# A group of seven products for chunk c3 of the first feed-forward's up projection, with the row sums, gates and tables moved around it

## The chip, the cores and the metric

The kernel runs on one core of a Trainium2 chip. The metric is the device time of one execution in microseconds (us). For the kernel before, three runs gave 896.94, 897.80 and 899.82 us; their median is 897.8 us. A further execution was taken with the hardware profiler; it took 896.07 us, and all views of the profile come from it.

## What is computed

The reference is a trunk of two layers over 256 rows of 1024 channels, in fp32. Each layer adds half a SwiGLU feed-forward, then a token mixer (a convolution module in the first layer, latent attention in the second), then half a second feed-forward:

```python
def swiglu_ffn(h, w1, w3, w2):
    return (jax.nn.silu(h @ w1) * (h @ w3)) @ w2
...
    h = h + FFN_RES_WEIGHT * swiglu_ffn(rmsnorm(h, ffn_norm1[i]), ffn1_w1[i], ffn1_w3[i], ffn1_w2[i])
    m = rmsnorm(h, mix_norm[i])
```

There are four feed-forwards, of which the change touches the first. Its first product, called up here, multiplies 256x1024 rows by w1 and by w3, each 1024x2816; its second product, called down, multiplies 256x2816 gates by w2, 2816x1024.

## The kernel before, in words

**The arithmetic.** TensorE multiplies in a reduced fp32 format, so that every operand is split in a high and a low part, and each product is made of three matmuls: `mm3` issues, in this order, the high part of the rows by the low part of the weights (L332), high by high (L335) and the low part of the rows by the high part of the weights (L336). ScalarE makes the high part of a weight (a copy that rounds), VectorE the low part (the raw weight less the high part).

**The weights.** They come from memory as blocks of 1 MB, 128 partitions by 2048 numbers, in the order of the list `blocks`. `load` fetches a block through SyncE's queue into one of four raw buffers (`RAW_BUFS`, pool `raw`; issue at L238), casts the high part in two halves on ScalarE (L246) and subtracts for the low part in two halves on VectorE (L247), into one of five pairs of weight buffers (`W_BUFS`). A raw buffer is free again when its low part is made. `weights` asks for the block that is used next, and `load_ahead` keeps a few blocks under way. `behind` holds these casts behind the last few instructions that are marked `urgent` on the same engine, and `order(a, b)` puts instruction a behind b; beyond that, the scheduler of the framework sets each engine's order when the program is built, and each engine, and SyncE's queue of transfers, works through its own order.

**The up projection** runs in chunks c0 to c5 (`ffn_in`, loop over c). A chunk yields 512 columns of w1 and of w3 for both halves of the rows (tb 0 and 1): four banks of 128x512, four weight blocks, 96 matmuls of 128x512 (c5 has half of that). Blocks are numbered b0, b1, ... here: c1 uses b4 to b7, c2 b8 to b11. Behind a chunk come its gates: Silu on ScalarE (L956), the product with the other bank on VectorE (L958, or L258 where it is `urgent`), and `turn`: VectorE transposes within 32x32 squares (L478), four transfers write the result to device memory (L482, gd<-gt) and one reads it back turned (L487, rows<-gd or gb<-gd), ScalarE and VectorE split it into the gates Gh and Gl (L853). The gates of c0 and c1 are read back into the tile `rows4`.

**A group of seven.** A chunk that stands in `SEVEN_UP` makes its 2x2 blocks of product (two halves of the rows, two halves of the inner dimension, w1 and w3) from seven block products instead of eight. It is Strassen's scheme in the form of Winograd. For it the rows need four sums and differences, `sums_of_rows` (L344 on VectorE), of rows that `whole_rows` puts together from high and low part first (L349, into a raw buffer), and each of them is split again by `forms_of` (L361 on ScalarE, L364 on VectorE). The weights need four differences of raw blocks, 128x2048 each, on VectorE (L200, raw<-raw,raw); `load_seven` fetches the four raw blocks (L184), makes these differences, the high halves (L214) and the low halves (L200, lo<-raw,hi). `seven_products` issues the seven products of 12 matmuls; between them it copies two banks (L258 on ScalarE) and makes two additions on VectorE (L258, u<-u,p), which are `urgent`. Its products are called first to seventh here; the fifth adds to the bank that the first addition reads. In the kernel before, c3 of the second, third and fourth feed-forward are such groups, and in all four feed-forwards the first four block columns of down are one (`SEVEN_DOWN`, `o.seven`), whose row sums are taken from `rows4`, that is from the gates of c0 and c1.

**Around it in the first feed-forward.** `diagonals` is a generator whose steps `beside` calls between products: it makes the convolution's diagonal matrices on ScalarE, 128x64 at a time (L1679, dpair). `rope_tables` makes sines and cosines of the positions on VectorE (L1366 and after) and ScalarE (L1398 to L1400), for the attention of the second layer. `Plain` makes the rows for the convolution behind down: squares (L429), a Sigmoid of one column (L669), which brings the table of that function in ahead of its use, and the scaling (L678).

## Time and profile before

| what | us |
|---|---|
| median of three runs | 897.8 |
| profiled execution, own time | 896.07 |
| its span (first to last instruction) | 894.3 |
| VectorE, busy | 743.1 |
| ScalarE, busy | 571.8 |
| low halves of ordinary blocks (L247), 236 of them, busy | 276.2 |
| low halves of groups (L200), 98 of them, busy | 115.6 |
| differences of raw blocks (L200), 28 of them, busy | 63.9 |

The span is taken from the trace; 1.77 us of the execution's own time lie around it. In the profile an engine is named PE (TensorE), DVE (VectorE), ACT (ScalarE), POOL (GpSimd) or SP (SyncE). A row of a timeline has the start in us from the span's beginning, the duration, engine, line and operation, the tile written and the tiles read, the size, and, where the engine was idle before it, the idle time and what ended it. "x2" stands for two instructions in one row. Durations of neighbours overlap a little, so the distance of two starts tells what an instruction costs in a full queue. A row of the windows has the busy time of each engine in a stretch, its number of instructions, and the clock that TensorE was granted (1.00 is full).

### The profile page before, as it was taken

What the parts mean: (1) busy time and instruction counts of PE and PEld (TensorE: products, weight loads), DVE (VectorE), ACT (ScalarE), POOL (GpSimd) and SP (SyncE); (2) the same over time, 40 slices, a digit from 0 to 9 for tenths busy, and PEclk for the clock granted to TensorE, in tenths of its full rate; (3) what the DMA queues carried; (4) which work ended last, traced back from release to release, by engine and by line L of the source; (5) the groups of instructions that cost most, each with busy time, mean ns of one, the idle gap of its engine ahead of it and who ended that gap; (6) DMA issues with size and microseconds to landing.
All of it is one profiled execution on the core that took longest, in us unless ns stands there. A gap on an engine that the chain in (4) does not pass through costs nothing.

```text
span 894.3 us, 12241 instructions
## 1 busy us (share of the span) xinstructions
PE 886.9 (99%) x4221; PEld 745.9 (83%) x4221; DVE 743.1 (83%) x1083; ACT 571.8 (64%) x993; POOL 104.2 (12%) x227
## 2 busy tenths in 40 slices
PE   9999999999999999999999999999999999999997
PEld 7888888898988888888888888888899888888886
DVE  6787789579998999999588989995768579989973
ACT  7966458488886646667375566673677566474752
POOL 1000000069962000000010000001400010000000
PEclk9999999999999999999999999999999999999999
DMA  9987629834215864939759369495635349378541
GB/s 330 375 303 274 232 59 355 295 121 172 106 60 194 289 258 144 374 109 388 259 175 339 118 218 357 123 392 182 223 142 189 141 154 342 104 260 317 180 196 48
DMA packets 71055, 198.94 MB, mean 222 GB/s; under 512 B 12369, under 2 KB 41937, under 8 KB 51665
## 3 DMA queue, kind: packets, MB, share of 16 engines
q1 hardware_dynamic: 70560, 197.47, 61.8%
q8 instruction: 33, 0.54, 0.2%
q10 hardware_dynamic: 432, 0.69, 0.2%
q14 instruction: 30, 0.24, 0.1%
HBM read 181.87 MB, written 16.25 MB: 222 GB/s over the span
## 4 chain that ended last, share of the span: by engine, by line
PE 92%; DVE 4%; ACT 2%; DMA 1%; issue 0%; SPq 0%; POOL 0%; DVEq 0%; ACTq 0%
PE u L336 16%; PE u L335 16%; PE u L332 16%; PE o L335 9%; PE o L336 9%; PE o L332 9%; PE gate L1005 2%; PE u L411 2%; DVE acc L1094 2%; PE u L1005 2%; PE tp L446 1%; PE a L335 1%; PE a L332 1%; PE a L336 1%; PE nope L336 1%; PE nope L332 1%
## 5 line engine op out<-in xcount | busy, mean ns | idle before, releaser
L247 DVE TENSOR_TENSOR lo<-raw,hi 128x1024 fp32r<-128x1024 f32 (+1 forms) x236 | 276.2, 1212 | 38.8 <-ACT hi L246 37.6
L246 ACT CAST hi<-raw 128x1024 fp32r<-128x1024 f32 (+1 forms) x238 | 236.8, 1044 | 89.3 <-DMA raw<-in_f2w 30.8
L332 PE MATMUL u<-lo,Xh 128*128 128x512 f32 x612 | 238.4, 389 | 0.1
L336 PE MATMUL u<-hi,Xl 128*128 128x512 f32 x612 | 238.3, 389 | 0.0
L335 PE MATMUL u<-hi,Xh 128*128 128x512 f32 x612 | 238.1, 389 | 0.0
L332 PEld LDWEIGHTS u<-lo,Xh 128*128 128x128 f32 x612 | 114.9, 188 | 24.5 <-ACT Xh L598 0.5
L336 PEld LDWEIGHTS u<-hi,Xl 128*128 128x128 f32 x612 | 114.9, 188 | 24.3 <-DVE Xl L465 0.5
L335 PEld LDWEIGHTS u<-hi,Xh 128*128 128x128 f32 x612 | 114.9, 188 | 23.8
L214 ACT CAST hi<-raw 128x1024 fp32r<-128x1024 f32 x98 | 97.7, 1050 | 51.8 <-DVE raw L200 44.9
L200 DVE TENSOR_TENSOR lo<-raw,hi 128x1024 fp32r<-128x1024 f32 x98 | 115.6, 1216 | 7.1 <-ACT hi L214 7.1
L332 PE MATMUL o<-lo,Gh 128*128 128x512 f32 (+1 forms) x276 | 106.6, 386 | 0.0
L335 PE MATMUL o<-hi,Gh 128*128 128x512 f32 (+1 forms) x276 | 106.5, 386 | 0.0
L336 PE MATMUL o<-hi,Gl 128*128 128x512 f32 (+1 forms) x276 | 106.5, 386 | 0.0
L437 POOL TENSOR_TENSOR ms<-ss 128x1 f32<-128x1 f32 x16 | 8.1, 510 | 597.6 <-ACT junk L429 597.6
L200 DVE TENSOR_TENSOR raw<-raw,raw 128x2048 f32<-128x2048 f32 x28 | 63.9, 2283 | 1.8 <-DMA raw<-in_f2w 0.9
L332 PEld LDWEIGHTS o<-lo,Gh 128*128 128x128 f32 x276 | 51.8, 188 | 10.5
L335 PEld LDWEIGHTS o<-hi,Gh 128*128 128x128 f32 x276 | 51.9, 188 | 10.5
L336 PEld LDWEIGHTS o<-hi,Gl 128*128 128x128 f32 x276 | 51.8, 188 | 10.4
L1094 DVE SCALAR_TENSOR_TENSOR acc<-V,dw,acc 128x128 f32<-128x128 f32 (+1 forms) x174 | 53.9, 391 | 0.0
L1115 ACT ACTIVATE prod<-V,dw 128x128 f32<-128x128 f32 (+1 forms) x128 | 45.6, 415 | 1.8 <-POOL Y L1116 1.0
L956 ACT ACTIVATE s<-u,R 128x512 f32<-128x512 f32 (+1 forms) x48 | 30.9, 647 | 24.8 <-PE u L336 24.1
L797 DVE SCALAR_TENSOR_TENSOR h<-o,rh,h 128x512 f32<-128x512 f32 (+1 forms) x18 | 12.9, 719 | 29.2 <-PE o L336 29.2
(265 smaller groups left out, 1257.7 us busy)
## 6 DMA issues: line engine op xcount, KB each, us to landing
raw<-in_f2w SPq DMA_DIRECT2D x66, 1024.0 KB, 6.2
raw<-in_f1w SPq DMA_DIRECT2D x62, 1024.0 KB, 6.5
raw<-in_cw SPq DMA_DIRECT2D x12, 1024.0 KB, 5.5
gd<-gt SPq DMA_DIRECT2D x160, 64.0 KB, 3.0
gb<-gd SPq DMA_DIRECT2D x24, 256.0 KB, 2.8
rows<-gd SPq DMA_DIRECT2D x16, 256.0 KB, 4.4
raw<-in_wo SPq DMA_DIRECT2D x4, 1024.0 KB, 4.9
hd<-rows SPq DMA_DIRECT2D x56, 64.0 KB, 2.4
```

Source lines behind the costliest of these rows:

```text
L200: ins = nc.vector.tensor_sub(out, left, right)
L214: casts[n, i] = nc.scalar.copy(hi[:, c], raw[:, c]), sub(lo[:, c], raw[:, c], hi[:, c].bitcast(F32))
L246: casts[len(loaded), i] = (nc.scalar.copy(hi[:, c], raw[:, c]), low.tensor_sub(lo[:, c], raw[:, c], hi[:, c].bitcast(F32)))
L247: low.tensor_sub(lo[:, c], raw[:, c], hi[:, c].bitcast(F32)))
L332: mm = nc.tensor.matmul(o, ah, bl, start=start, stop=False, skip_group_check=seeded)
L335: nc.tensor.matmul(o, ah, bh, start=False, stop=False, skip_group_check=seeded)
L336: return nc.tensor.matmul(o, al, bh, start=False, stop=stop, skip_group_check=seeded)
L411: mm = nc.tensor.matmul(o, al if kind == "x" else ah, bl if kind == "l" else bh, start=start and n == 0, stop=stop and n == len(kinds) - 1)
L956: nc.scalar.activation(s[:, :w], u[0, tb][:, :w], AF.Silu, scale=X.r[tb])
L1005: mm = nc.tensor.matmul(u[:, t], w[:, c], X.x[:, k, t], start=(k == 0), stop=(k == KT - 1))
L1094: dve_last.append(nc.vector.scalar_tensor_tensor(out if j == j1 - 1 else y, v, w, y, op0=ALU.mult, op1=ALU.add))
L1115: prods_last.append(nc.scalar.activation(p, v, AF.Copy, scale=w))
```

## The change

c3 of the first feed-forward becomes a group of seven (`SEVEN_UP[0]`), so it has 84 matmuls instead of 96. With it go:

- `whole_rows` is called at c1 for the first feed-forward, as for the others (two chunks ahead of the group), and there it stands behind the last low half of block b5 (`after`). The forms are kept in the part of Gh and Gl that later chunks fill.
- The row sums of the down group and its first form are made ahead of the group at c3 in the first feed-forward (`down`), instead of at c5.
- The gates of c2's first half of the rows (tb 0) are not held behind the group's copy and addition there (`held`); those of the second half are, as in the other groups, and their low part also stands behind the seventh product's.
- Each diagonal stands behind the latest high half that has been issued.
- `rope_tables` is no longer called behind the third feed-forward (from where the scheduler had placed its instructions in the first feed-forward's up projection), but as the last step of `diagonals`; its first instruction stands behind a low half of a block of down. The Sigmoid of `Plain` stands behind its last sine.

```diff
@@ -46,7 +46,7 @@
 
 
 
-SEVEN_UP = {1: (3,), 2: (3,), 3: (3,)}
+SEVEN_UP = {0: (3,), 1: (3,), 2: (3,), 3: (3,)}
 SEVEN_DOWN = (0, 1, 2, 3)
 
 CONV_DVE = (0, 2, 4)
@@ -344,9 +344,11 @@
             nc.vector.tensor_tensor(out, left, right, op=op)
         return sorted(((n, out) for n, out, *_ in sums), key=lambda s: s[0])
 
-    def whole_rows(xh, xl):
+    def whole_rows(xh, xl, after=()):
         x = rawp.tile([P, HB], F32, tag="raw", name=uid("xs")).rearrange("p (k t) -> p k t", t=S)
-        nc.vector.tensor_add(x, xh.bitcast(F32), xl.bitcast(F32))
+        whole = nc.vector.tensor_add(x, xh.bitcast(F32), xl.bitcast(F32))
+        for a in after:
+            order(whole, a.ins)
         return [x[:, 4 * a:4 * a + 4, tbs(tb)] for tb in range(2) for a in range(2)]
 
     def forms_of(sums, sh, sl, late={}):
@@ -365,7 +367,7 @@
             out[n] = [z[:, i].rearrange("p (k t) -> p k t", t=P) for z in (sh, sl)]
         return out
 
-    def seven_products(xh, xl, forms, banks, late={}):
+    def seven_products(xh, xl, forms, banks, late={}, held=True):
 
 
         def rows(a, tb):
@@ -393,8 +395,10 @@
         add = urgent(nc.vector.tensor_add)(c12, c21, kept)
         order(casts[n0 + 5, 0][1], add.ins)
         for high, low in gates[-NT:] if not late else ():
-            order(high, last.ins)
-            order(low, add.ins)
+            if held:
+                order(high, last.ins)
+                order(low, add.ins)
+            held = True
         low_gates = [low for high, low in gates[-NT:] if not late]
         product(rows(1, 0), c11, False)
         product(forms[2], c21, False)
@@ -666,7 +670,9 @@
             if tb == 0 and i == 1:
                 self.sq = sq
 
-                nc.scalar.activation(small.tile([P, 1], F32, tag="silu", name="sigm"), self.ss[0][:, 1:], AF.Sigmoid)
+                table = nc.scalar.activation(small.tile([P, 1], F32, tag="silu", name="sigm"), self.ss[0][:, 1:],
+                                             AF.Sigmoid)
+                order(table, tables[-1].ins)
 
         @urgent
         def scale(self, tb):
@@ -840,7 +846,7 @@
             return ffn_in(act, X, make_next, beside, apart, SEVEN_UP.get(n, ()), n in SEVEN_DOWN)
 
     def ffn_in(act, X, make_next, beside, apart, seven_up, seven_down):
-        first_form = {}
+        down_sums, first_form = [], {}
         Gh = act.tile([P, NF, S], F32R, tag="Gh", name=uid("Gh"))
         Gl = act.tile([P, NF, S], F32R, tag="Gl", name=uid("Gl"))
         def turn(c, tb, w, g):
@@ -881,6 +887,13 @@
                         last = mm
                 last = mm
 
+        def down():
+
+            z11, z21, z12, z22 = (rows4[:, n, :] for n in range(4))
+            down_sums.extend(sums_of_rows(z11, z12, z21, z22))
+            first_form.update(forms_of(down_sums[:1], *(act.tile([P, 2, S], F32R, tag=tag, name=uid(tag))
+                                                        for tag in ("s1h", "s1l"))))
+
         for c in range(6):
 
             both = c == 5
@@ -889,19 +902,17 @@
             u = {}
             if c == 0 and X.pool:
                 first_chunk(X, u)
-            if seven_up and c == min(seven_up) - (1 if X.whole else 2):
-                forms = forms_of(sums_of_rows(*whole_rows(X.xh, X.xl)), Gh[:, 14:], Gl[:, 14:])
+            if seven_up and c == min(seven_up) - 2:
+                after = [casts[5, PIECES - 1][1]] if X.whole else ()
+                forms = forms_of(sums_of_rows(*whole_rows(X.xh, X.xl, after)), Gh[:, 14:], Gl[:, 14:])
+            if c == 3 if X.whole else both:
+                down()
             if c in seven_up:
                 for key in ((0, 0), (0, 1), (1, 1), (1, 0)):
                     u[key] = bank("A", "u")
-                seven_products(X.xh, X.xl, forms, {(tb, m): b for (m, tb), b in u.items()})
+                seven_products(X.xh, X.xl, forms, {(tb, m): b for (m, tb), b in u.items()}, held=not X.whole)
                 beside()
                 beside()
-            if both and seven_down:
-                z11, z21, z12, z22 = (rows4[:, n, :] for n in range(4))
-                down_sums = sums_of_rows(z11, z12, z21, z22)
-                first_form = forms_of(down_sums[:1], *(act.tile([P, 2, S], F32R, tag=tag, name=uid(tag))
-                                                       for tag in ("s1h", "s1l")))
             for m in range(0 if u else 1 if both else 2):
                 parts = weights(KT // kn, c > 0 or m > 0)
                 before = None
@@ -1357,13 +1368,13 @@
         return nxt
 
 
-    def rope_tables():
+    def rope_tables(first):
         pi = const.tile([P, NT], I32, name="pi")
         fetch(pi, pos)
         fr = const.tile([P, 32], F32, name="fr")
         fetch(fr, invf)
         pf = const.tile([P, NT], F32, name="pf")
-        nc.vector.tensor_copy(pf, pi)
+        order(nc.vector.tensor_copy(pf, pi), first.ins)
         ang = const.tile([P, NT, 32], F32, name="ang")
         for tb in range(NT):
             nc.vector.tensor_scalar(ang[:, tb, :], fr, pf[:, tb:tb + 1], None, op0=ALU.mult)
@@ -1397,8 +1408,7 @@
         for i in range(2):
             nc.scalar.activation(cc[:, :, i, :], ra3, AF.Sin)
         nc.scalar.activation(sn[:, :, 0, :], r3, AF.Sin, scale=-1.0)
-        nc.scalar.activation(sn[:, :, 1, :], r3, AF.Sin)
-        return cc, sn
+        return cc, sn, nc.scalar.activation(sn[:, :, 1, :], r3, AF.Sin)
 
     def rope(pool, dst, src, n, cc, sn, tb, after=()):
 
@@ -1676,7 +1686,8 @@
         nc.gpsimd.tensor_tensor(ident2, ident[:, :64], ident[:, 64:], op=ALU.add)
         for g in (1, 0):
             for j in range(KP - g):
-                nc.scalar.activation(dpair[g][:, j, :], ident2, AF.Copy, scale=wp2[:, g, j:j + 1])
+                diagonal = nc.scalar.activation(dpair[g][:, j, :], ident2, AF.Copy, scale=wp2[:, g, j:j + 1])
+                order(diagonal, casts[len(loaded) - 1, PIECES - 1][0].ins)
                 if j % 4 == 3:
                     yield
             if g == 1:
@@ -1684,6 +1695,8 @@
                 while "down" not in stage:
                     yield
         nc.scalar.activation(ident2, ident2, AF.Copy, scale=wp2[:, 1, KP - 1:])
+        yield
+        tables.extend(rope_tables(casts[n_used[0] + 1, PIECES - 1][1]))
 
     class Rows512:
 
@@ -1696,6 +1709,7 @@
     rows = Rows512()
 
     stage = []
+    tables = []
     todo = diagonals()
 
     def beside():
@@ -1712,7 +1726,7 @@
     apart.close()
     X = ffn(X, lambda act: Norm("ffn1_1", half=True, turn_by_dma=rows), apart=True)
     X = ffn(X, lambda act: Norm("mix_1", turn_by_dma=rows), apart=True)
-    cc, sn = rope_tables()
+    cc, sn, _ = tables
     X = mla(X, lambda act: Norm("ffn2_1", half=True, turn_by_dma=rows), cc, sn)
     ffn(X, Final)
 
```

## Prediction

> **What bounds the kernel now.** I read first the page's busy times and clock and the chain that ended last, then timelines (start and duration in us, engine, line) of TensorE (PE) and VectorE (DVE), and for the changed kernel the order in which each engine's instructions are built.
>
> ```profile
> span 894.3 us, 12241 instructions
> ...
> PE 886.9 (99%) x4221; PEld 745.9 (83%) x4221; DVE 743.1 (83%) x1083; ACT 571.8 (64%) x993; POOL 104.2 (12%) x227
> ...
> PEclk9999999999999999999999999999999999999999
> ...
> PE 92%; DVE 4%; ACT 2%; DMA 1%; issue 0%; SPq 0%; POOL 0%; DVEq 0%; ACTq 0%
> ```
>
> TensorE works 886.9 of 894.3 us at the full clock in every slice, and the chain that ended last is 92% TensorE. So the time is the number of matmuls times their pitch, plus whatever makes TensorE wait. VectorE is at 83% as an average; how near it is to its limit has to be seen stage by stage.
>
> ```profile
> 27.98 0.39 PE L332 MATMUL u<-lo,Xh 128*128 128x512 f32 x1
> ```
>
> ```profile
> 57.67 0.39 PE L336 MATMUL u<-hi,Xl 128*128 128x512 f32 x1
> ```
>
> 27.98 is the first matmul of chunk c1 of the first feed-forward, 57.67 the 132nd: 131 pitches in 29.69 us, 0.2267 us each. Chunks c1 and c2 have 96 matmuls each, so c3, the one that changes, begins at 27.98 + 192 x 0.2267 = 71.5; I call this T0.
>
> ```profile
> 40.00:60.00 20.00, 20.00 (x90) 16.57 (x89) 17.38 (x24) 16.27 (x25) 0.00 (x0) 1.00 0.89 307
> 60.00:80.00 20.00, 20.00 (x90) 16.58 (x89) 16.44 (x20) 10.44 (x15) 0.00 (x0) 1.00 0.85 301
> ```
>
> In both stretches TensorE is busy for all 20 us at clock 1.00, while VectorE has only 2.6 and 3.6 us free, just ahead of the stage that gets more work for it.
>
> **The change part by part.**
>
> *TensorE.* c3 is now seven block products of 12 matmuls instead of eight: 84 instead of 96. Gain: 12 x 0.2267 = **2.72 us**, 0.30% of the time. All else of TensorE's order stays.
>
> *VectorE's new work.* The second feed-forward already has such a group; its timeline gives every price (a price is the distance of two starts, since a start follows the last with no pause).
>
> ```profile
> 331.82 2.29 DVE L200 TENSOR_TENSOR raw<-raw,raw 128x2048 f32<-128x2048 f32 x1
> ...
> 335.36 1.22 DVE L200 TENSOR_TENSOR lo<-raw,hi 128x1024 fp32r<-128x1024 f32 x1
> 336.49 0.69 DVE L344 TENSOR_TENSOR rows<-rows 128x512 f32<-128x512 f32 x1
> 337.09 1.22 DVE L200 TENSOR_TENSOR lo<-raw,hi 128x1024 fp32r<-128x1024 f32 x1
> 338.23 0.69 DVE L364 TENSOR_TENSOR s1l<-rows,s1h 128x512 fp32r<-128x512 f32 x1
> 338.83 0.68 DVE L344 TENSOR_TENSOR rows<-rows 128x512 f32<-128x512 f32 x1
> 339.44 0.68 DVE L258 TENSOR_TENSOR s<-s,u 128x512 f32<-128x512 f32 x1
> 340.15 0.71 DVE L478 STREAM_TRANSPOSE gt<-s 128x512 f32<-128x512 f32 x1
> 340.78 0.65 DVE L258 TENSOR_TENSOR s<-s,u 128x512 f32<-128x512 f32 x1
> 341.36 2.35 DVE L200 TENSOR_TENSOR lo<-raw,hi 128x1024 fp32r<-128x1024 f32 x2
> ...
> 344.94 2.36 DVE L200 TENSOR_TENSOR lo<-raw,hi 128x1024 fp32r<-128x1024 f32 x2 [0.62 <-ACT hi L214]
> 348.83 0.70 DVE L258 TENSOR_TENSOR u<-u,p 128x512 f32<-128x512 f32 x1 [1.53 <-PE u L336]
> 349.44 0.68 DVE L853 TENSOR_TENSOR Gl<-gb,Gh 128x512 fp32r<-128x512 f32 x1
> 350.03 1.22 DVE L200 TENSOR_TENSOR lo<-raw,hi 128x1024 fp32r<-128x1024 f32 x1
> 351.17 2.29 DVE L200 TENSOR_TENSOR raw<-raw,raw 128x2048 f32<-128x2048 f32 x1
> 353.37 1.22 DVE L200 TENSOR_TENSOR lo<-raw,hi 128x1024 fp32r<-128x1024 f32 x1
> 354.51 0.69 DVE L258 TENSOR_TENSOR u<-u,p 128x512 f32<-128x512 f32 x1
> 355.11 2.35 DVE L200 TENSOR_TENSOR lo<-raw,hi 128x1024 fp32r<-128x1024 f32 x2
> 357.38 0.69 DVE L853 TENSOR_TENSOR Gl<-gb,Gh 128x512 fp32r<-128x512 f32 x1
> ```
>
> Half a block's low part 1.13 (335.36 to 336.49); a row sum L344 0.60 (336.49 to 337.09); a form's low part L364 0.60; a gate product (L258, s) 0.58 (340.78 to 341.36); a turn L478 0.63; the group's add (L258, u) 0.61; a gate's low part L853 0.59; a difference of two raw blocks 2.20 (351.17 to 353.37). The trace has the sum of whole rows (L349, 128x2048 too) only in other stages; I take 2.2. Added on VectorE: six low halves, four differences, one L349, four L344, four L364, two adds: 6.8 + 8.8 + 2.2 + 2.4 + 2.4 + 1.2 = 23.8 us. That is harmless only if it fits ahead of TensorE's need.
>
> *Before T0.*
>
> ```profile
> 29.54 2.34 DVE L247 TENSOR_TENSOR lo<-raw,hi 128x1024 fp32r<-128x1024 f32 x2
> 31.80 0.70 DVE L478 STREAM_TRANSPOSE gt<-s 128x512 f32<-128x512 f32 x1
> ```
>
> Block 5's low part ends where the turn starts, at 31.80; in the changed order L349 stands there. From L349 up to the instruction in front of c2's second gate product, VectorE's built order has 16 low halves, 1 L349, 3 differences, 5 L344, 4 L364, 4 L853, 3 turns and 3 gate products: 18.1 + 2.2 + 6.6 + 3.0 + 2.4 + 2.4 + 1.9 + 1.7 = 38.3 us, so they are done at 70.1 if nothing is waited for. The next instruction waits for c2's last matmul until T0 + 0.2 = 71.7 anyway: **1.6 us of slack**. On the way each low part is early: block 6's is done at 36.9 and wanted at 38.9 (27.98 + 48 x 0.2267), the group's first at 58.9, wanted at 71.5. Cost 0, if the data come in time (rival C).
>
> *From T0 on, TensorE waits.*
>
> ```profile
> 93.03 0.39 PE L336 MATMUL u<-hi,Xl 128*128 128x512 f32 x1
> ```
>
> ```profile
> 93.46 0.69 DVE L958 TENSOR_TENSOR s<-s,u 128x512 f32<-128x512 f32 x1 [0.65 <-PE u L336]
> ```
>
> The matmul that starts at 93.03 for 0.39 releases VectorE at 93.46, 0.04 later; so c2's second gate product starts at about T0 + 0.2. In the built order the group's third to seventh low parts all stand **behind** this product. First come the product, two turns, six low halves (products 3 to 5, counted from 1), three L344 and one L364: 0.58 + 1.26 + 6.79 + 1.80 + 0.60 = 11.03, so to T0 + 11.23. Then the first add, 0.61; a difference, 2.20; two low halves, 2.26; L853, 0.59; the second add, 0.61; two low halves, 2.27; L853, 0.59; and the first low half of the next chunk's first block, 1.13: 10.26, and 0.1 until that last one has landed: T0 + 21.6. TensorE, unhindered, would want this block at T0 + 84 x 0.2267 = T0 + 19.05. **TensorE waits 2.6 us** in all. Stepwise: the fifth product adds into the bank that the first add reads, and that add ends at T0 + 11.9 where TensorE asks at T0 + 10.9 (1.1 us); the sixth product's low part comes 0.6 after TensorE's later asking, the seventh's 0.7, the next block's 0.2.
>
> The second feed-forward's group, for comparison:
>
> ```profile
> 343.12 0.39 PE L332 MATMUL u<-lo,Gh 128*128 128x512 f32 x1
> ```
>
> Its second product starts at 343.12, so its T0 is 343.12 - 2.72 = 340.40. There three L344, the form, two low halves and the first turn (335.36 to 340.15) stand ahead of the second gate product, and VectorE still idles 0.62 us (ahead of 344.94) and 1.53 us (ahead of the first add). The seventh product's first low half is done near 356.3 (355.11 + 1.13 and the landing), and TensorE takes it up at 340.40 + 72 x 0.2267 = 356.72: 0.4 us to spare, 2.55 us of room in all. The changed chunk has two low halves, three L344, one L364 and one turn more behind T0: 2.26 + 1.80 + 0.60 + 0.63 = 5.3 us; its gate product starts 0.2 us sooner after T0 (340.78 is T0 + 0.38). 5.3 - 2.55 - 0.2 = 2.55 us of waiting: the same by a second way. Bounds: nothing (rival B), and, if all 22 instructions took what they overlap too (1.22 for 1.13, up to 0.09 each), 2 us more, 4.6. I take 2.6, on which both ways agree.
>
> *What I cost at nothing.* ScalarE gets six high halves, four form casts and two copies more; its free time in the rows above (3.7 and 9.6 of 20 us) hides them.
>
> ```profile
> 45.82 0.39 ACT L1398 ACTIVATE cc<-red_abs 128x64 f32<-128x64 f32 x2
> ```
>
> ```profile
> 179.31 1.28 ACT L669 ACT_TABLE_LOAD   x1
> ...
> 180.71 0.71 ACT L678 ACTIVATE hn<-h,R 128x512 f32<-128x512 f32 x1
> ```
>
> The four sines go from ScalarE's early part to just ahead of the Sigmoid table load at 179.31, where two of them may delay that load; nothing of TensorE waits there now, and the rows of the next stage are scaled from 180.71 on. Bounds: 0, and 0.4 us (two sines in the row at 45.82) if the load is on the path; I take 0. VectorE's rope arithmetic leaves the first stage for the end of the down stage, the diagonals are spread four at a time behind high casts: both leave the crowded stretch after 31 us, where TensorE has no pause that could go, so they gain nothing by themselves. The sums of rows for the down group run at chunk c3 instead of c5: VectorE is lighter later, TensorE had no pause there either: 0.
>
> *SyncE.* L349's result takes one of four raw buffers from 31.8 to about 50.2, so each block of c2 is fetched one release later, and block 7's fetch comes behind the first turn's four writes, at about 31.2 us.
>
> ```profile
> raw<-in_f1w SPq DMA_DIRECT2D x62, 1024.0 KB, 6.5
> ...
> gd<-gt SPq DMA_DIRECT2D x160, 64.0 KB, 3.0
> ...
> rows<-gd SPq DMA_DIRECT2D x16, 256.0 KB, 4.4
> ```
>
> By the median 6.5 us it lands at 37.7, and its high half takes 1 us more; VectorE asks for it at 37.5. Those 1.2 us fall into the slack of 1.6, and TensorE wants this block at 44.3.
>
> *Sum.* -2.72 + 2.6 + 0 = **-0.1 us**. The profiled execution's own time is 896.07 (span 894.3 and 1.77 around it), so I expect 895.9 to 896.1 for such a one; the median of the runs shown is 1.7 above it, 897.8, so the forecast on that scale is **897.7**.
>
> *A rule beside it.* The clock row shows full speed in all slices, and in the two windows quoted TensorE had no free time at all. The Trainium skill, page "TensorE: Matmul & The Clock Gate", section "A second HAM failure mode: psum-queue depth-cycling", states that a TensorE which pauses shortly but often between groups of matmuls can swing between half and full clock. That speaks against this change, which makes four such pauses in 11 us; no trace here shows it. It makes rival E.
>
> **The rivals.**
>
> A, the forecast: the gain is given back by waits in the same group. For: the order is fixed, and the sum of its prices is longer than TensorE's 19.05. 897.7; with the upper bound, 4.6 waited, 899.7.
>
> B, VectorE keeps up, as in the second feed-forward, which has no waits: full gain, 897.8 - 2.7 = 895.1. Against it: there the sums and the low halves of one more product stand ahead of T0, and the changed order has no place for them.
>
> C, slower: VectorE is late already at T0, since rows of c1 come late through memory. The sums L344 of c1's gates need c1's turned rows; VectorE's chain asks for the second one (L853) at 65.6.
>
> ```profile
> 54.16 0.71 DVE L478 STREAM_TRANSPOSE gt<-s 128x512 f32<-128x512 f32 x1
> ...
> 69.67 0.69 DVE L853 TENSOR_TENSOR Gl<-rows,Gh 128x512 fp32r<-128x512 f32 x1
> ```
>
> Now this pair, c1's second turn and its L853, lies 15.5 us apart. In the changed order the turn ends at 57.7; with the page's medians 3.0 + 4.4 its rows are there at 65.1, in time; with 15.5 us they come at 73.2, and L853, a difference, the first gate product and L344 bring VectorE to 73.2 + 0.59 + 2.20 + 0.58 + 0.60 = 77.2, 5.5 us behind 71.7. It decides from 1.6 us of lateness on (landing past about 67), and then each us costs one. Against it: in SyncE's changed order no fetch of a block stands between the turn and its read-back, as now three do. Its middle, half way between 1.6 and 5.5 us of what it may cost: 3.5 us, 901.2.
>
> D, a delay where the convolution begins, by the sines: +0.4 us, 898.1.
>
> E, the clock falls to half at the first wait and comes back at the end of the group: the last 36 to 48 matmuls at twice the pitch, 8 to 11 us: about 907. For it speaks no row: the clock is full throughout, but TensorE hardly pauses now.
>
> That the change does not do what it says can be left out: the built order has 12 matmuls fewer, and all of it stands in the first feed-forward.
>
> **How the numbers follow.** A measurement of this kernel tells about 0.3% (2.7 us) from no change. Chances: A 0.70, B 0.10, C 0.15, D 0.02, E 0.03. B lies at the bound itself: 0.07 of it faster, 0.03 within. C: 0.12 slower, 0.03 within; A loses 0.03 to slower, where its upper bound meets a late landing. Faster 0.07, within 0.3% 0.75, slower 0.18. The range goes from B's lower half, 895.3, to C's middle, 901.2, leaving out some 0.17.
>
> **What would show it.** The group: 84 matmuls, T0 at 71.5, then pauses of TensorE of about 1.1, 0.6, 0.7 and 0.2 us at the fifth, sixth and seventh product and the next chunk's first, with VectorE's parts as the releaser (for the first of them the add L258), and VectorE without idle time from T0 + 0.2 to T0 + 21.6; c4 begins at about 71.5 + 21.6 = 93.1 instead of 93.3. If TensorE has no pause there, B is right. If VectorE idles in front of c1's L853 or a difference ahead of T0, and is past 71.7 with L344, C is. Granted clock under 1.00 in that stretch: E. A pause of TensorE at some other place, above all in the down group or after 180 us, would mean that I left out a cost.

## The result and the profile after

Over 22 runs of each, taken in turns on the same chips, the kernel before has a median of 896.67 us (895.23 to 899.82) and the changed kernel 897.70 us (896.00 to 901.21). The ratio is 1.0017, with a 95% interval of 1.0009 to 1.0024: the changed kernel is **1.5 us slower** (0.8 to 2.2). The forecast was 0.1 us faster. That the median of the changed kernel is 897.7, the figure of the forecast, is chance: the forecast stood on a median of 897.8 us for the kernel before, which with more runs is 896.67.

The page of the changed kernel's profile, its span, busy times and chain:

```profile
span 898.8 us, 12265 instructions
...
PE 886.5 (99%) x4209; PEld 743.3 (83%) x4209; DVE 765.3 (85%) x1104; ACT 579.5 (64%) x1005; POOL 104.9 (12%) x227
...
PE 78%; DMA 11%; DVE 7%; issue 1%; ACT 1%; SPq 1%; POOL 0%; DVEq 0%; ACTq 0%
```

VectorE (DVE) has 22 us more to do, as summed up (765.3 against 743.1). The chain of work that ended last, 92% TensorE before, now has 7% VectorE, and transfers (DMA 11%). This execution took 900.59 us, one of the slowest of the 22, so its span is not to be set against the 894.3 of before: the stages have to be looked at one by one. Start of the group (T0), the products with a pause in front, and the first matmul of chunk c4, in TensorE's timeline:

```profile
71.29 0.39 PE L332 MATMUL u<-lo,Xh 128*128 128x512 f32 x1
...
78.15 0.50 PE L332 MATMUL u<-lo,Gh 128*128 128x512 f32 x1 [1.26 <-ACT u L258]
...
85.02 0.50 PE L332 MATMUL u<-lo,Gh 128*128 128x512 f32 x1 [1.13 <-DVE u L258]
...
88.34 0.50 PE L332 MATMUL u<-lo,Gh 128*128 128x512 f32 x1 [0.31 <-DVE lo L200]
...
91.81 0.50 PE L332 MATMUL u<-lo,Xh 128*128 128x512 f32 x1 [0.45 <-DVE lo L200]
...
94.69 0.49 PE L332 MATMUL u<-lo,Xh 128*128 128x512 f32 x1
```

c3 lasts from 71.29 to 94.69, 23.40 us, where 84 matmuls need 19.04: TensorE waits 4.36 us. The gain is 2.72, so the chunk is 1.6 us longer than the 96 matmuls of before, which is as much as the measured 1.5. In brackets stand the pauses: in front of the third product 1.26 us, for a copy of ScalarE (ACT); of the fifth, 1.13, for the addition; of the sixth and seventh, 0.31 and 0.45, for low halves. (A pause costs 0.2 to 0.3 us more than its idle time, since the matmuls around it are further apart than usual.)

Two stretches by busy time, 71.4 to 93 us (c3, in the changed kernel but for its last 1.7 us) and 93 to 142 us (c4, c5 and most of the down group), changed kernel first, then the kernel before (columns: stretch, PE, PEld, DVE, ACT, POOL busy with their counts, PEclk, share and GB/s of DMA):

```profile
71.40:93.00 21.60, 18.44 (x78) 13.99 (x77) 21.60 (x25) 15.99 (x22) 0.00 (x0) 1.00 0.52 165
93.00:142.00 49.00, 49.00 (x218) 40.33 (x217) 46.78 (x48) 32.57 (x51) 0.00 (x0) 1.00 0.67 236
```

```profile
71.40:93.00 21.60, 21.60 (x97) 17.90 (x96) 16.30 (x20) 12.64 (x21) 0.00 (x0) 1.00 0.71 250
93.00:142.00 49.00, 49.00 (x218) 40.56 (x217) 38.74 (x39) 30.55 (x55) 0.00 (x0) 1.00 0.46 155
```

VectorE has not one free moment in the 21.6 us, and 2.2 us in the 49 behind them; before, it had 5.3 and 10.3. The granted clock is 1.00 in all of them.

Where VectorE fell behind is seen in its timeline around T0:

```profile
66.66 0.69 DVE L859 TENSOR_TENSOR Gl<-rows,Gh 128x512 fp32r<-128x512 f32 x1
69.26 0.69 DVE L859 TENSOR_TENSOR Gl<-rows,Gh 128x512 fp32r<-128x512 f32 x1 [1.92 <-ACT Gh L859]
69.87 2.29 DVE L200 TENSOR_TENSOR raw<-raw,raw 128x2048 f32<-128x2048 f32 x1
72.07 0.68 DVE L258 TENSOR_TENSOR s<-s,u 128x512 f32<-128x512 f32 x1
72.67 0.69 DVE L344 TENSOR_TENSOR rows<-rows 128x512 f32<-128x512 f32 x1
73.27 0.68 DVE L258 TENSOR_TENSOR s<-s,u 128x512 f32<-128x512 f32 x1
...
84.27 0.69 DVE L258 TENSOR_TENSOR u<-u,p 128x512 f32<-128x512 f32 x1
```

At 66.66 and 69.26 stand the low parts of c1's two gates, forecast for 65.6 and 66.2. In front of the second one VectorE idled 1.92 us. So the second gate product of c2, forecast for T0 + 0.2, began at 73.27, T0 + 1.98, and the rest of the chain follows it with the forecast durations: the first addition ends at 84.96, 11.7 us behind the start of that product (forecast 11.7).

What it idled for is a transfer. SyncE's issues (its queue works through them in this order):

```profile
50.37 2.74 SPq L184 DMA_DIRECT2D raw<-in_f1w  x2
54.00 2.34 SPq L486 DMA_DIRECT2D gd<-gt  x4
56.44 0.65 SPq L184 DMA_DIRECT2D raw<-in_f1w  x1
58.73 0.78 SPq L486 DMA_DIRECT2D gd<-gt  x2
62.04 0.34 SPq L491 DMA_DIRECT2D rows<-gd  x1
62.43 0.90 SPq L486 DMA_DIRECT2D gd<-gt  x2
65.97 0.34 SPq L491 DMA_DIRECT2D rows<-gd  x1
```

At 50.37 to 53.1 two raw blocks of the group are fetched, at 54.00 to 56.3 c1's first turn is written, at 56.44 the last raw block is fetched, at 58.73 two of the four writes of c1's second turn. The first two blocks landed at 58.6 and 61.2, so the first turn's writes behind them only at 61.4 to 62.0. At 62.04 their read-back could go; SyncE had held two writes of the second turn behind it, which therefore started at 62.43. They landed at 65.9, the second read-back was issued at 65.97 and landed at 68.58. This hold in SyncE's queue is the smaller part of the delay: the two writes of the second turn that were not held landed only at 64.7 and 64.9, just behind the fetch issued at 56.44 (64.45), and the held ones 1.0 us after them. From issue to landing the eight writes took 3.0 to 7.4 us, 6.3 as a median, where the forecast had 3.0; the two read-backs took 3.4 and 2.6, where it had 4.4. ScalarE's timeline shows the same from the other side:

```profile
65.50 0.62 ACT L859 CAST Gh<-rows 128x512 fp32r<-128x512 f32 x1 [1.27 <-DMA rows<-gd]
68.61 0.62 ACT L859 CAST Gh<-rows 128x512 fp32r<-128x512 f32 x1 [2.48 <-DMA rows<-gd]
72.24 2.00 ACT L214 CAST hi<-raw 128x1024 fp32r<-128x1024 f32 x2 [3.02 <-DVE raw L200]
74.15 1.06 ACT L1689 ACTIVATE dpair<-dpair,wpair 128x64 f32<-128x64 f32 x4
75.11 1.98 ACT L214 CAST hi<-raw 128x1024 fp32r<-128x1024 f32 x2
77.00 0.61 ACT L363 CAST s1h<-rows 128x512 fp32r<-128x512 f32 x1
77.52 0.58 ACT L258 COPY u<-u 128x512 f32<-128x512 f32 x1
```

ScalarE waits 2.48 us for the rows (68.61), then 3.02 us for the difference of raw blocks that VectorE makes behind them (72.24), and then it has high halves of two products, diagonals and a form in its queue ahead of the copy at 77.52, for which TensorE waits until 78.15. The copy itself needed only the first product, which ended about 74.2.

### The profile page after: what moved, and what is told of

It reads as the page before. It is cut to its first block, busy times and chain, and to the rows that moved or that the text cites. A ratio compares the mean times of both kernels' runs of the same rounds, so it can differ in the third digit from the quotient of the medians.

```text
span 898.8 us, 12265 instructions
## 1 busy us (share of the span) xinstructions
PE 886.5 (99%) x4209; PEld 743.3 (83%) x4209; DVE 765.3 (85%) x1104; ACT 579.5 (64%) x1005; POOL 104.9 (12%) x227
## 4 chain that ended last, share of the span: by engine, by line
PE 78%; DMA 11%; DVE 7%; issue 1%; ACT 1%; SPq 1%; POOL 0%; DVEq 0%; ACTq 0%
PE u L332 11%; PE u L336 11%; PE u L335 11%; PE o L336 9%; PE o L332 9%; PE o L335 9%; DMA raw<-in_f1w 4%; PE u L1016 3%; PE gate L1016 3%; DMA gd<-gt 2%; DMA raw<-in_f2w 2%; DVE lo L200 2%; DVE lo L247 1%; PE o L1252 1%; DVE raw L200 1%
## 5 line engine op out<-in xcount | busy, mean ns | idle before, releaser
L247 DVE TENSOR_TENSOR lo<-raw,hi 128x1024 fp32r<-128x1024 f32 (+1 forms) x228 | 266.2, 1209 | 29.5 <-ACT hi L246 28.6
L246 ACT CAST hi<-raw 128x1024 fp32r<-128x1024 f32 (+1 forms) x230 | 228.2, 1043 | 74.9 <-DMA raw<-in_f2w 30.2
L332 PE MATMUL u<-lo,Xh 128*128 128x512 f32 x592 | 230.9, 390 | 1.7 <-DVE lo L200 1.7
L336 PE MATMUL u<-hi,Xl 128*128 128x512 f32 x592 | 230.5, 389 | 0.0
L335 PE MATMUL u<-hi,Xh 128*128 128x512 f32 x592 | 230.4, 389 | 0.0
L214 ACT CAST hi<-raw 128x1024 fp32r<-128x1024 f32 x112 | 111.6, 1049 | 52.6 <-DVE raw L200 44.2
L200 DVE TENSOR_TENSOR lo<-raw,hi 128x1024 fp32r<-128x1024 f32 x112 | 132.0, 1212 | 6.0 <-ACT hi L214 6.0
L332 PEld LDWEIGHTS u<-lo,Xh 128*128 128x128 f32 x592 | 111.1, 188 | 26.0 <-DVE lo L200 2.6
L336 PEld LDWEIGHTS u<-hi,Xl 128*128 128x128 f32 x592 | 111.1, 188 | 23.5 <-DVE Xl L469 0.4
L200 DVE TENSOR_TENSOR raw<-raw,raw 128x2048 f32<-128x2048 f32 x32 | 73.0, 2281 | 1.0 <-DMA raw<-in_f2w 0.7
```

Source lines behind the costliest of these rows:

```text
L200: ins = nc.vector.tensor_sub(out, left, right)
L214: casts[n, i] = nc.scalar.copy(hi[:, c], raw[:, c]), sub(lo[:, c], raw[:, c], hi[:, c].bitcast(F32))
L246: casts[len(loaded), i] = (nc.scalar.copy(hi[:, c], raw[:, c]), low.tensor_sub(lo[:, c], raw[:, c], hi[:, c].bitcast(F32)))
L247: low.tensor_sub(lo[:, c], raw[:, c], hi[:, c].bitcast(F32)))
L332: mm = nc.tensor.matmul(o, ah, bl, start=start, stop=False, skip_group_check=seeded)
L335: nc.tensor.matmul(o, ah, bh, start=False, stop=False, skip_group_check=seeded)
```

## The experiments

Theory 1, after these readings: VectorE's queue is the bound of the stage from T0 to the down group, and the 1.8 us of waits beyond the forecast come from its late start, for c1's rows. Rivals: the loss lies elsewhere, in later stages (theory 2); GpSimd could take the work without slowing VectorE, or not (theory 3); what is gained in the up group is lost in the down group (rival 4). Each kernel was timed against the kernel before on the same chip, in five rounds; microseconds are the ratio's distance from 1 times 897. "Waits" are the stretch's length in that kernel's profile less its matmuls times 0.2267. The edits are shown shortened: names such as `third_difference` or `seventh_low` stand for that instruction, and each order is set in the first feed-forward alone.

**1. Gates of c1 behind the third product's difference**

```diff
+    for _, low in gates[2:4]:
+        order(low, third_difference.ins)
```

> The low parts of the gates of c1 stand behind the difference of raw blocks for the third product, so VectorE does not idle in front of them. Theory 1 (VectorE reached the second gate product of c2 1.7 us late because it waited for the turned rows of c1): the product starts at T0 + 0.2 again, and the waits of TensorE in the group fall from 4.2 to about 3.1 us (one row sum now stands behind the first addition, which costs 0.6 again); against the kernel before +0.4 us. Theory 2 (the group's loss is not VectorE's lateness, but the loss lies in later stages, where the profile of the changed kernel has 2 us of waits in the second feed-forward): the time stays at +1.5 us.

Measured: ratio 1.0006 (0.9997 to 1.0015), +0.5 us. VectorE's and TensorE's timelines:

```profile
65.71 2.29 DVE L202 TENSOR_TENSOR raw<-raw,raw 128x2048 f32<-128x2048 f32 x1
67.92 1.28 DVE L862 TENSOR_TENSOR Gl<-rows,Gh 128x512 fp32r<-128x512 f32 x2
69.12 0.68 DVE L261 TENSOR_TENSOR s<-s,u 128x512 f32<-128x512 f32 x1
71.12 0.69 DVE L261 TENSOR_TENSOR s<-s,u 128x512 f32<-128x512 f32 x1 [1.32 <-PE u L339]
```

```profile
PE u L335 <- DVE lo L202: 1.4, 2, 1.1
PE u L335 <- DVE u L261: 0.9, 1, 0.9
```

VectorE now idles for TensorE (1.32 us) ahead of the second gate product, which starts at T0 + 0.20 (T0 = 70.92). c3 lasts 22.23 us, 3.19 of them waits (3.1 expected). The pause of the third product is gone with it, though nothing was done to ScalarE. Theory 1 holds, theory 2 does not. This rests on the waits: the intervals of this kernel and of the changed one overlap, so that the times alone do not settle it.

**2. Row sums and first form of the down group behind the seventh product**

```diff
+    for ins in sum_ins:
+        order(ins, seventh_low.ins)
```

`sum_ins` are the four L344 of the down group.

> The four row sums and the first form of the down group stand behind the low part of the seventh product; the gates of c1 stay where they are. Theory 1: VectorE's chain is 2.4 us shorter behind the second gate product and the product starts 0.6 us sooner, but is still about 1 us late; waits of TensorE in the group 1.8 us instead of 4.2; against the kernel before -0.9 us. Theory 2: less than 1 us gained over the changed kernel, so +0.5 us or more.

Measured: 0.9997 (0.9986 to 1.0007), -0.3 us. c3 waits 1.69 us, as expected (1.8); but the down group, which has no waits in the changed kernel's profile, now has 1.04. From T0 to the end of the down group it is 73.59 us, against 75.23 in the changed kernel and 73.44 before.

**3. Both**

The edits of 1 and of 2 together.

> Both: the gates of c1 behind the third product's difference, and the row sums and form of the down group behind the seventh product. Theory 1: VectorE is in time at T0 and its chain is T0 + 19.8 long against 19.05 of TensorE; waits 0.7 us; against the kernel before -2.0 us. Theory 2: no better than +0.5 us.

Measured: 1.0001 (0.9993 to 1.0010), +0.1 us; a miss. VectorE was in time, but c3 waits 2.23 us and the down group 1.04. The built order had changed at other places too: half of the sixth product's low part stood ahead of the last difference, so the seventh product's high part came late (VectorE idled 0.76 us for it), and a row sum and a gate product stood ahead of c4's first low half.

**4. Tables and diagonals alone, without the group**

```diff
-SEVEN_UP = {0: (3,), 1: (3,), 2: (3,), 3: (3,)}
+SEVEN_UP = {1: (3,), 2: (3,), 3: (3,)}
-            if c == 3 if X.whole else both:
+            if both:
```

> The changed kernel without the group of seven in the first feed-forward: only diagonals, rope tables and the Sigmoid behind the sines are moved. Theory 1: no difference to the kernel before (within 0.3 us). Theory 2 (the moved tables disturb the start of the convolution and the stages behind it): +0.5 to +1.5 us.

Measured: 0.9998 (0.9989 to 1.0006). No difference beyond the interval (-1.0 to +0.5 us): without the group, the moved tables, diagonals and the Sigmoid cost nothing that shows.

**5 and 6. GpSimd takes work from VectorE**

```diff
-            down_sums.extend(sums_of_rows(z11, z12, z21, z22))
+            down_sums.extend(sums_of_rows(z11, z12, z21, z22, nc.gpsimd))
...
-            gates.append((nc.scalar.copy(gh, bv), nc.vector.tensor_sub(low, bv, gh.bitcast(F32))))
+            gates.append((nc.scalar.copy(gh, bv), eng.tensor_sub(low, bv, gh.bitcast(F32))))
```

Here `eng` is GpSimd for c1, and `forms_of` takes it for the first form; experiment 6 does the same for the row sums and forms of the up group.

> The changed kernel, with the low parts of the gates of c1, the four row sums of the down group and its first form's low part made by GpSimd instead of VectorE (seven instructions of 128x512). Theory 1 (VectorE's queue is the bound of the group): its chain from T0 is T0 + 18.6 long against 19.05 of TensorE, and it does not wait for c1's rows; no wait of TensorE in the group; against the kernel before -2.4 us (some tenths lost in the down group, which starts sooner). Theory 3 (work on GpSimd slows VectorE as much as it relieves it): no better than the kernel before.

> As the last, and the four row sums and four form low parts of the up group on GpSimd too. Theory 1: no wait in the group either, VectorE has 4.8 us more room ahead of T0; same as the last, -2.4 to -2.7 us against the kernel before. Theory 3: slower than the last.

Measured: 1.0042 (1.0028 to 1.0056), +3.8 us, and 1.0075 (1.0056 to 1.0094), +6.7 us. Both slower; theory 1's numbers missed and theory 3 holds. Experiment 5, VectorE, then GpSimd (POOL):

```profile
65.75 3.27 DVE L200 TENSOR_TENSOR raw<-raw,raw 128x2048 f32<-128x2048 f32 x1
...
75.82 7.34 DVE L200 TENSOR_TENSOR lo<-raw,hi 128x1024 fp32r<-128x1024 f32 x5
```

```profile
67.62 2.56 POOL L860 TENSOR_TENSOR Gl<-rows,Gh 128x512 fp32r<-128x512 f32 x1 [0.75 <-ACT Gh L860]
...
72.88 1.31 POOL L366 TENSOR_TENSOR s1l<-rows,s1h 128x512 fp32r<-128x512 f32 x1
```

The difference that takes 2.28 us beside an idle GpSimd takes 3.27 here, five low halves 7.34 instead of 5.72 (experiment 2 has them at 5.72), and an instruction of GpSimd 2.56 us, where one that starts beside an idle VectorE takes 1.31 (72.88; VectorE is idle until 73.19). The Trainium skill, page "SBUF — State Buffer", section "Who interferes with whom", says that an instruction of VectorE with two inputs from the on-chip memory contends with GpSimd's reads; all the instructions here are of that kind, and the rows agree. Waits in c3: 3.39 us. The profiled execution of experiment 5 is the fastest of its twelve, so that its profile does not show all of the 3.8 us.

**7. The changed kernel again**

No edit; a second profile and a second set of runs.

> The changed kernel once more, for a second profile. Theory 1: waits of 4.2 us in the first feed-forward's group again, and none in the second feed-forward's group, as in the other four profiles: +1.0 to +1.5 us against the kernel before. Theory 2 (the waits of 2 us in the second feed-forward come with the change): they are there again.

Measured: 1.0018 (1.0007 to 1.0029), +1.6 us. c3 waits 4.07 us. The second feed-forward's group, however, has waits in both profiles of the changed kernel; of the first one:

```profile
PE u L332 <- DVE lo L200: 1.6, 2, 1.3
```

(0.8 us in experiment 7.) The profile of before has none there, nor have experiments 1 to 5; 6 and 12 have some, and 4, 8, 9 and 11 have such waits in the fourth feed-forward, experiment 4 without being slower over its runs. So not every execution has such waits, and the first group's 1.6 us account for the measured 1.5 without them. But the two profiled executions of the changed kernel took 900.59 and 899.84 us, where the medians of their sets are 897.70 and 898.82, and both have these waits in the second feed-forward. How often each kernel has them, and whether the change makes them more frequent, is left open.

**8. The group alone**

```diff
-SEVEN_UP = {1: (3,), 2: (3,), 3: (3,)}
+SEVEN_UP = {0: (3,), 1: (3,), 2: (3,), 3: (3,)}
```

This one line is changed in the kernel before, and nothing else.

> The kernel before with the group of seven alone: tables and diagonals stay early, row sums one chunk ahead, gates held. Theory 1: VectorE has some 4 us of rope arithmetic more in the stretch after 31 us, and gets further behind at T0; waits 6 to 9 us in the group, so +3 to +6 us against the kernel before.

Measured: 1.0072 (1.0055 to 1.0088), +6.5 us: 7.81 us of c3 beyond its matmuls at full pitch, and 1.6 in the down group. Part of it is the clock:

```profile
76.24 0.39 PE L336 MATMUL u<-hi,Gl 128*128 128x512 f32 x1
79.50 0.50 PE L332 MATMUL u<-lo,Gh 128*128 128x512 f32 x1 [2.88 <-DVE lo L200]
...
81.60 0.63 PE L332 MATMUL u<-lo,Gh 128*128 128x512 f32 x1
```

```profile
80.30:83.60 3.30, 3.30 (x9) 0.50 0.33 84
```

After a pause of 3.0 us (79.50 less 76.24 and a pitch), the granted clock is 0.50 from 80.3 to 83.6 us; eight matmuls are 0.43 apart, 1.6 us lost.

**9. A better order on VectorE**

```diff
+    order(sixth_low.ins, last_difference.ins)
+    for ins in sum_ins:
+        order(ins, b20_low.ins)
+    for _, low in gates[4:6]:
+        order(low, b19_low.ins)
```

The edit of 1 is in it too; b19 and b20 are c4's first two blocks, `gates[4:6]` the gates of c2.

> All on VectorE, with a better order: the gates of c1 behind the third product's difference, the last difference ahead of the sixth product's low part, the gates' low parts of c2 behind the low part of the next chunk's first block, and the down group's row sums and first form behind the second block of c4. Theory 1: the chain from T0 is T0 + 18.9, so no wait in the up group (2.7 us gained by the start of c4); but VectorE has the same work up to the down group, which now starts sooner, so 0.5 to 1.5 us of it are waited for there, as seen at 139 us in the second and third experiment; against the kernel before -1.2 to -2.2 us. Rival 4 (the gain in the up group is given back in full by the down group): 0.

Measured: 1.0005 (0.9994 to 1.0016), +0.4 us. TensorE's waits from T0 to the end of the down group:

```profile
PE o L335 <- DVE o L261: 1.0, 1, 1.0
PE o L335 <- DVE lo L202: 1.0, 2, 0.6
PE u L335 <- DVE lo L202: 1.0, 1, 1.0
```

The up group waits 1.26 us in all (0 expected), so c4 starts 1.46 us sooner than with eight products. The wait is for the seventh product, whose high part was late by ScalarE's queue:

```profile
85.38 0.62 ACT L863 CAST Gh<-gb 128x512 fp32r<-128x512 f32 x1 [2.60 <-DMA gb<-gd]
...
86.49 1.98 ACT L217 CAST hi<-raw 128x1024 fp32r<-128x1024 f32 x2
```

VectorE had made the difference for it by 83.1, but in ScalarE's queue the high part stood behind a cast of c2's gates, for which ScalarE waited 2.60 us: again an instruction that waits for rows from memory, ahead of one that TensorE needs. The down group (o) then waits 3.13 us. Rival 4 is right in this execution: the group's gain is given back 40 us later.

**10 and 12. Without the down group's row sums**

```diff
-            down_sums.extend(sums_of_rows(z11, z12, z21, z22))
+            down_sums.extend([(0, z22), (1, z11), (2, z21), (3, z12)])
```

Experiment 10 has the edit of 1 beside it, experiment 12 the edits of 9, with the form that is left in the place of the sums. Both leave out the four sums and so compute something else in the down group.

> The first experiment, with the four row sums of the down group left out in the first feed-forward (the products there use rows that are not summed). It is 2.4 us less work on VectorE between T0 and the down group. Theory 1: the chain from T0 is about 0.2 + 0.6 + 1.3 + 6.8 + 0.6 + 2.2 + 2.3 + 0.6 + 0.6 + 2.3 + 0.6 + 1.2 = 19.3, so 0.3 us of wait in the up group, and less than 0.5 in the down group: -2 us or more against the kernel before. Rival 4: 0.

Measured: 1.0004 (0.9992 to 1.0017). The test did not separate the theories: without the sums the first form reads c1's rows directly, and the scheduler put it ahead of the third product's difference, so that VectorE idled 3.73 us for these rows; c3 waits 3.87 us, 1.3 of them for the second product, whose bank is read by a gate product of VectorE that was late; the down group waits 0.75.

> The order of the ninth experiment, with the four row sums of the down group left out in the first feed-forward (the products there use rows that are not summed), and the form that is left kept behind the second block of c4, so that nothing ahead of the group waits for c1's rows. VectorE has 2.4 us less to do between T0 and the end of the down group. Theory 1 (the amount of VectorE's work up to the down group is the bound): c4 starts 1.7 us sooner than in the kernel before, as in the ninth experiment, and of the 3.1 us waited for in the down group there, 2.4 are gone: -1.0 us at the end of the down group, -1 us in the time. Rival 4a (the down group waits for something else, a transfer or the place of its sums): 3 us are waited for in the down group again, +1 us or more at its end.

Measured: 0.9993 (0.9982 to 1.0005), -0.6 us. c3 waits 1.31 us, the down group 2.39, where 0.7 were expected and 3.13 stood in experiment 9.

```profile
PE u L335 <- DVE lo L202: 1.0, 1, 1.0
PE o L335 <- ACT o L261: 0.9, 1, 0.9
PE o L335 <- DVE lo L202: 0.4, 1, 0.4
```

Of 2.4 us of work taken from VectorE, 0.7 us of waiting went. The longest wait of the down group is now for a copy of ScalarE, and VectorE idles 1.58 us for a high half and 1.29 us for a raw block behind 105 us. So the amount of VectorE's work is not the whole bound of the down group; neither theory's number came out. What else it hangs on (the fetches, which wait for raw buffers that VectorE frees, or ScalarE's queue) was not taken apart.

**11. Tables early again**

```diff
-        order(nc.vector.tensor_copy(pf, pi), first.ins)
+        nc.vector.tensor_copy(pf, pi)
```

`rope_tables` is called where it was in the kernel before, and the Sigmoid is no longer held behind its sines.

> The changed kernel with the rope tables made early again, as in the kernel before; diagonals stay spread. Theory 1: some 20 small instructions of VectorE, about 3 us in all, come into the stretch ahead of T0 and the group; part of it falls into the 2 us that VectorE idles for c1's rows: 1 to 3 us later than the changed kernel, +2.5 to +4.5 us against the kernel before. Rival (where the tables are made does not matter): +1.5 us.

Measured: 1.0045 (1.0032 to 1.0059), +4.0 us. In the profile c3 is 7.93 us beyond its matmuls, with the clock at 0.50 from 95.2 to 98.5 us, behind a pause of 2.7 us. Where the tables are made costs nothing without the group (experiment 4) and 2.5 us with it (4.0 less 1.5).

The main ones in one table, from the profiles (us): waits in c3, waits in the down group, T0 to the end of the down group (73.44 before), and the measured difference.

| kernel | c3 | down | T0 to end | measured |
|---|---|---|---|---|
| changed | 4.36 | 0.00 | 75.23 | +1.5 |
| 1 | 3.19 | 0.00 | 74.04 | +0.5 |
| 2 | 1.69 | 1.04 | 73.59 | -0.3 |
| 3 | 2.23 | 1.04 | 74.16 | +0.1 |
| 5 | 3.39 | 1.33 | 75.57 | +3.8 |
| 7 | 4.07 | 0.27 | 75.24 | +1.6 |
| 8 | 7.81 | 1.58 | 80.24 | +6.5 |
| 9 | 1.26 | 3.13 | 75.11 | +0.4 |
| 12 | 1.31 | 2.39 | 74.42 | -0.6 |

No version is faster than the kernel before by more than its interval. The waits are read from one execution each, the measured difference from all. They disagree most in experiments 9 and 12, where T0 to the end is 1.7 and 1.0 us longer than before and +0.4 and -0.6 us were measured: their profiled executions took 899.40 and 898.50 us, where the medians are 898.31 and 896.61. So the waits of their down groups may be larger than is usual, and what was read from them above holds for these executions.

## Why the prediction was wrong

**The gain** was right: 84 matmuls, 2.72 us.

**The group's waits of 2.6 us** were right for what they were worked out for, a VectorE that is in time at T0. Experiment 1 has this case: the fifth product's pause is 1.1 us, the sixth's 0.5 (0.6 forecast), and the seventh's 1.2, of which 0.6 is a row sum that the edit put there (0.7 forecast). The prices and the order that is built were enough for it.

**The step that failed is "Before T0": "Cost 0, if the data come in time", with 1.6 us of slack.** They did not come in time. The rows of c1 were put at 65.1 by adding the medians of a write and a read-back, 3.0 + 4.4 us, to the end of the turn. In fact they landed at 68.58: from the end of the turn (58.7, where 57.7 was forecast) it took 9.9 us instead of 7.4. The term that was mis-sized is the write, 7.2 us instead of 3.0, since it lies behind a fetch of 1 MB that was issued 2.3 us ahead of it, and since SyncE's queue holds the last two of its four transfers behind the first turn's read-back (1.0 us of the 7.2); the read-back took 2.6 us instead of 4.4. VectorE reached the second gate product at T0 + 1.98, where the forecast's sum gives T0 - 1.4, 3.4 us later: 1.9 of them idle for these rows, 0.6 idle for a high half at 56.2, the rest small gaps. Without the wait for the rows, the other 1.5 would have stayed within the slack of 1.6; with it the product came 1.8 us late, and the waits were 4.36 instead of 2.6. Undoing this one wait (experiment 1) takes off 1.2 us of waits, though a row sum that moved with it costs 0.6, and about 1.0 us of the time.

**Rival C** was this mechanism, with its deciding point (landing past about 67) and its price (each microsecond beyond it costs one). What I held against it, that no fetch stands between the turn and its read-back, looked at the wrong thing: the fetches in front of the turn delay it as well. Its chance of 0.15 was too low, and the size of 3.5 us too large: 1.8.

**"What I cost at nothing", ScalarE's casts,** was wrong in place. Its free time hides the work as an amount; but a high half that waits for VectorE's late difference holds the copy behind it, and the third product waited 1.26 us for this copy, a pause that the forecast did not have. In experiment 1 it is gone, so it adds no second cause.

**The sums of the down group** were said to move from c5 to c3, and VectorE to be lighter later. In the built order of the kernel before they stand at c3 already (four L344 between 70.87 and 77.33 in its timeline); the call moved and the instructions did not. It changed no term of the sum.

**Tables and diagonals at nothing** was right without the group (experiment 4), but with it their place counts: early tables cost 2.5 us more (experiment 11), and the group alone 6.5 (experiment 8).

**Rival E**, the clock, was wrong at these pauses: it stayed at 1.00 through four of 0.3 to 1.3 us. By the rule of the Trainium skill that the prediction cites, frequent short pauses could have let it swing; the rows do not bear that out here.

## What to carry to other kernels

In a stage where one engine's queue is full, a sum of durations along its built order gives the waits to some tenths, but only from a point where the engine is known to be in time, and while no other queue is late (in experiments 3 and 9 the sums missed by 1.5 and 1.3 us); for what arrives by transfer, follow the queue that issues it, one entry after another, with everything in flight ahead of it, and do not add medians. An instruction that waits for memory belongs behind those for which the bottleneck waits: here one such order was worth about 1.0 us of a loss of 1.5. And a gain of matmuls in one group is only kept if the next stage that needs the same engine is ready sooner too: in the profiles of experiments 2, 9 and 12, c4 starts 1.0 to 1.5 us sooner, and all of it is lost again by the end of the down group 40 us later.

## What the runs showed of the hardware

The granted clock fell to half in three runs, behind pauses of TensorE of 3.0 us (experiment 8), 2.7 us (experiment 11) and 3.4 us (experiment 6), each time for 3.4 us. The rows of experiments 6 and 11:

```profile
89.60:92.90 3.30, 3.06 (x7) 0.50 0.90 295
```

```profile
95.20:98.50 3.30, 3.30 (x10) 0.50 0.87 305
```

Another pause, of 2.5 us (experiment 6, from 78.1 us), left it at 1.00. The length of a pause is not all that decides, as these traces have it. In experiments 8, 11 and 6 the clock first rises at 5.19, 6.44 and 4.20 us and falls at 80.28, 95.19 and 89.53 us, that is 22, 26 and 25 times 3.413 us later. Divided into stretches of that length, the stretch that ends with the fall has TensorE idle for 2.6, 2.6 and 3.0 us of its 3.4 (a matmul counted with the 0.39 us of its row), while the pause of 2.5 us lies in two stretches, with 0.8 us of it in one and 1.55 in the next. So what counts here seems to be how much of a pause falls into one such stretch; no run was made to test that. The Trainium skill, page "TensorE: Matmul & The Clock Gate", section "What's actually happening", gives about 3.4 us of idling in a window that runs freely. The traces agree with the window; in these runs less idling was enough.

GpSimd beside VectorE: a VectorE difference of 128x2048 took 3.27 us instead of 2.28, a GpSimd instruction of 128x512 up to 2.56 instead of 1.31 (experiment 5). The kernels that hand VectorE's work to an idle GpSimd are 3.8 and 6.7 us slower than the kernel before.
